# Branch A's gate product by blocks of two with seven products, its sums added in HBM

## The chip, the cores and the metric

The kernel runs on one core of a Trainium2 chip. The metric is the device time of one execution in microseconds (us). The core has engines that run beside one another, each through its own queue in order: TensorE (PE in the profile) multiplies matrices, VectorE (DVE) and ScalarE (ACT) work elementwise, GpSimd (POOL) does elementwise work too, and SyncE (SP) issues transfers (DMA) between HBM and on-chip memory. A matmul's result goes to PSUM, in banks of 128 x 512 floats; everything else lies in SBUF as tiles of 128 partitions.

## The reference

A two-layer backbone over 1024 latent tokens of 1024 channels (batch 1) and 256 context tokens. The even layer, which the change touches, is

```python
def even_mixer(h, h0, p):
    z = h @ p["w_in"]                       # 1024 -> 5 x 1024
    va, vg, ga, xb, gb = jnp.split(z, ...)
    y_a = conformer_conv(va, vg, p) * jax.nn.silu(ga)
    y_b, hT = rglru_branch(xb, p, h0, True)
    y_b = y_b * jax.nn.silu(gb)
    return jnp.concatenate([y_a, y_b], axis=-1) @ p["w_out"], hT
```

`conformer_conv` is a gate `va * sigmoid(vg)`, a depthwise convolution of width 31, a LayerNorm over the channels and a SiLU. `h` is the input after an RMS norm and a modulation. The odd layer (pooling mixer C) follows and is not changed. All is float32.

## The kernel before

Activations lie with channels on partitions: eight tiles of 128 channels x 1024 tokens, and each token half (512) is one PSUM bank. A float32 product is made of three matmuls of rounded operands: a number is split into a high part (`...h`, a cast on ACT to the format that PE reads) and a low part (`...l`, the difference, formed on POOL or DVE), and high x high, high x low and low x high are summed in one bank. `mm3_fixed` and `prod` are this loop over blocks of 128 channels.

The stages in order of the program: the condition and modulation sums; then eight *rounds*, one for each tile of channels, with the products `vg`, `va`, `xb` and the recurrence's gates on PE, the convolution on DVE, and the recurrence spread over DVE, ACT and POOL (`l` tiles); then the product `gb`; `wob`, the half of the output projection that reads branch B (eight output tiles x 48 matmuls); then `ga`, the gate of branch A, eight output tiles x two token halves x 24 matmuls; then `woa`, the half of the output projection that reads branch A, and the odd layer.

`woa` is already done by blocks of two with seven products (Strassen in Winograd's form): two output tiles, two halves of the contracted channels and two token halves form 2 x 2 blocks, and seven products of 12 matmuls take the place of eight. Its operands are called `b11`, `t1`, `t2`, `b21`, `t3`, `b22`, `t4`, its weights 1 to 7; sums and differences of activations (`ya`) and of weights are formed on DVE. Three banks `a`, `c`, `b` take the products, and bank `b` begins as a copy of bank `a` after product 1, made on ACT.

What sets the order: up to the flag `fixed[0] = False` the helpers `on`, `act`, `cast`, `vec` and `gp` tie each instruction to the one before on its engine, so that the order written out in the program is each engine's order. Their line in the profile is L670 (of the helper `on`). Behind the flag a scheduler orders by priority; `tc.high_priority(offset=EVAC)` moves an instruction ahead, `tc.issue_after` holds it behind another.

Around the change, before: in `wob`'s last two tiles ACT and DVE form the LayerNorm's sums (`mu`, `lsq`, `lnsum`); PE sums them over the channels with a matrix of ones (`ms_ln`); `ln_root` takes the root on ACT, `ln_scale` the reciprocal and eight scalings of `u` on DVE, `ln_silu` eight SiLUs on ACT, each for both token halves. The first two gate tiles (0 and 4) are written in the fixed order, with the row sum of half 1 behind the first of them; the other six follow in a loop (L161 to L163, L1428 to L1439) that multiplies the SiLU of the gate onto `u`, forms the operands of `woa`, and has the modulation sums of the second layer (`mods`, L1386) placed between. The weights' low parts of `ga` are formed on POOL, 128 x 1024 each.

## Time and profile before

| what | us |
|---|---|
| median of three runs | 1268.59 |
| lowest and highest run | 1265.97, 1269.95 |
| span of the profiled execution | 1263.6 |
| PE / DVE / ACT / POOL busy | 1249.8 / 1139.3 / 653.8 / 295.7 |
| gate product `ga` on PE, first to last start | 578.9 to 666.2 |

The span is that of one execution on the chip; the times of the runs have some 5 us around it. Rows of the timeline give start, duration, engine, source line, operation, output tile, input tiles, shapes and a count; in brackets stands how long the engine was idle before and for what. Groups give how often, the busy time and the mean in ns. Waits give total, times and longest. The granted clock of TensorE is full in all 40 slices.

### The profile page before, as it was taken

How to read it: one execution, taken by the hardware profiler on the slowest of the kernel's cores; microseconds unless marked ns; L12 is line 12 of the kernel's file. 1: busy time of each engine (PE TensorE's matmuls, PEld its weight loads, DVE VectorE, ACT ScalarE, POOL GpSimd, SP SyncE). 2: the span in 40 equal slices, each digit the busy share in tenths (PEclk: the TensorE clock that was granted, in tenths of full speed). 3: DMA queues.
4: the chain of work that ended last, by engine and by line, in shares of the span. 5: the costliest groups of instructions: out<-in, count | busy, mean ns of one | idle time of the engine just before them, and what ended most of it. 6: DMA issues, size and time to landing. Idle time of an engine off the chain costs nothing.

```text
span 1263.6 us, 16209 instructions
## 1 busy us (share of the span) xinstructions
PE 1249.8 (99%) x5866; PEld 1035.6 (82%) x5866; DVE 1139.3 (90%) x1746; ACT 653.8 (52%) x952; POOL 295.7 (23%) x176
## 2 busy tenths in 40 slices
PE   9999999999999999999999999999999999999997
PEld 7788888888888888888887878888888888888786
DVE  7799999999999999998978969999899987977975
ACT  8464566656666534237535445744343444644642
POOL 0015364436444547543210023000000000000002
PEclk9999999999999999999999999999999999999999
DMA  9970121112121233442436666344323334759723
GB/s 376 388 254 33 52 65 46 63 43 75 42 84 42 84 119 132 159 150 84 147 112 225 202 206 183 103 136 148 125 94 140 117 125 126 268 199 335 285 71 134
DMA packets 78705, 182.29 MB, mean 144 GB/s; under 512 B 7712, under 2 KB 23328, under 8 KB 78624
## 3 DMA queue, kind: packets, MB, share of 16 engines
q1 hardware_dynamic: 67328, 172.33, 39.8%
q10 hardware_dynamic: 11296, 8.92, 2.2%
q8 instruction: 46, 0.75, 0.2%
q14 instruction: 35, 0.29, 0.1%
HBM read 137.18 MB, written 44.04 MB: 143 GB/s over the span
## 4 chain that ended last, share of the span: by engine, by line
PE 70%; DVE 18%; DMA 7%; issue 2%; ACT 2%; POOL 1%; SPq 0%; POOLq 0%; ACTq 0%; DVEq 0%
PE wob L670 7%; DVE conv L670 5%; PE va L670 5%; PE xb L670 4%; PE vg L670 4%; DVE l L670 3%; PE fold L670 3%; PE g L670 3%; PE qb_v L1153 2%; PE ga L670 2%; PE qb_g L1156 2%; PE ga L161 2%; PE qb_v L1156 2%; PE qb_g L1155 2%; PE qb_g L1153 2%
## 5 line engine op out<-in xcount | busy, mean ns | idle before, releaser
L670 DVE SCALAR_TENSOR_TENSOR conv<-u,sm,conv 128x505 f32<-128x505 f32 (+6 forms) x224 | 153.6, 744 | 1.0
L2045 POOL TENSOR_TENSOR o<-x,rr 128x256 f32<-128x256 f32 (+1 forms) x10 | 9.2, 952 | 448.4 <-ACT rr L2045 448.4
L670 ACT ACTIVATE l<-g,sm 128x512 f32<-128x512 f32 (+1 forms) x96 | 58.7, 619 | 57.7 <-PE g L670 57.0
L670 POOL TENSOR_TENSOR l<-l,l 128x1280 f32<-128x1280 f32 x16 | 47.1, 2967 | 25.6 <-ACT l L670 15.1
L670 PE MATMUL gb<-h0h,wl_gb 128*128 128x512 f32 x128 | 49.9, 390 | 0.4 <-POOL wl_gb L670 0.4
L670 PE MATMUL va<-h0h,wl_va 128*128 128x512 f32 x128 | 49.9, 390 | 0.2 <-DVE wl_va L670 0.2
L98 ACT CAST wq_g<-wr_g 128x512 fp32r<-128x512 f32 x48 | 28.2, 621 | 41.9 <-DMA wr_g<-wg 15.6
L670 PE MATMUL gb<-h0l,wh_gb 128*128 128x512 f32 x128 | 49.8, 389 | 0.0
L670 PE MATMUL gb<-h0h,wh_gb 128*128 128x512 f32 x128 | 49.8, 389 | 0.0
L670 PE MATMUL va<-h0l,wh_va 128*128 128x512 f32 x128 | 49.8, 389 | 0.0
L670 PE MATMUL va<-h0h,wh_va 128*128 128x512 f32 x128 | 49.8, 389 | 0.0
L670 PE MATMUL wob<-ybl,wh_wob 128*128 128x512 f32 x128 | 49.8, 389 | 0.0
L670 PE MATMUL wob<-ybh,wl_wob 128*128 128x512 f32 x128 | 49.8, 389 | 0.0
L670 PE MATMUL wob<-ybh,wh_wob 128*128 128x512 f32 x128 | 49.8, 389 | 0.0
L670 DVE TENSOR_TENSOR_SCAN l<-l,l 128x256 f32<-128x256 f32 (+1 forms) x32 | 48.7, 1521 | 1.1
L670 DVE SCALAR_TENSOR_TENSOR conv<-cL,wsum,conv 128x506 f32<-128x506 f32 (+3 forms) x70 | 48.1, 745 | 0.2
L670 POOL TENSOR_TENSOR l<-l,uc 128x1280 f32<-128x1280 f32 x16 | 47.6, 2999 | 0.0
L98 ACT CAST wq_wo<-wr_wo 128x512 fp32r<-128x512 f32 x48 | 28.6, 620 | 35.5 <-DVE wr_wo L1134 12.4
L98 ACT CAST wq_v<-wr_v 128x512 fp32r<-128x512 f32 x48 | 28.1, 620 | 33.7 <-DMA wr_v<-wfold 16.6
L670 PE MATMUL xb<-h0l,wh_xb 128*128 128x512 f32 x112 | 43.8, 391 | 0.0
L670 PE MATMUL xb<-h0h,wh_xb 128*128 128x512 f32 x112 | 43.8, 391 | 0.0
L670 POOL TENSOR_TENSOR wl_xb<-wr_xb,wh_xb 128x1024 fp32r<-128x1024 f32 x7 | 16.8, 2407 | 114.5 <-ACT wh_xb L670 114.5
(680 smaller groups left out, 4362.5 us busy)
## 6 DMA issues: line engine op xcount, KB each, us to landing
modw<-modW SPq DMA_DIRECT2D x16, 512.0 KB, 10.2
mod<-modT SPq DMA_DIRECT2D x32, 256.0 KB, 3.4
wr_v<-wfold SPq DMA_DIRECT2D x16, 512.0 KB, 4.0
wr_g<-wg SPq DMA_DIRECT2D x16, 512.0 KB, 4.3
wr_wo<-wo SPq DMA_DIRECT2D x16, 512.0 KB, 4.1
mod<-modT SPq DMA_DIRECT2D x14, 512.0 KB, 4.5
y_b<-y SPq DMA_DIRECT2D x24, 256.0 KB, 3.5
y_t<-y SPq DMA_DIRECT2D x24, 256.0 KB, 3.1
```

What stands on the lines that cost most here:

```text
L98: return (nc.scalar.copy(hi, src), eng.tensor_tensor(out=lo, in0=src, in1=hi.bitcast(F32), op=sub))
L161: mm(ps, hi[:, kc], xh[k][:, cols], start=(k == 0), stop=False)
L670: last[eng] = f(*args, **kw)
L1153: nc.tensor.matmul(ps, hi, xh[k], start=(first and k == 0), stop=False, skip_group_check=not first)
L1155: nc.tensor.matmul(ps, hi, xl[k], start=False, stop=False, skip_group_check=not first)
L1156: mm = nc.tensor.matmul(ps, lo, xh[k], start=False, stop=(k == KH - 1), skip_group_check=not first)
L2045: tail[eng] = f(*args, **kw)
```

## The change

The gate product is now made in four rows q of two output tiles (q and q + 4) by seven products each. The activations' operands are `h` in halves of its channels and tokens and four sums of them (`t1` to `t4`), the weights three of `w_in`'s blocks and four sums.

*Sums in HBM.* They are formed by transfers in the rounds. SP copies the high parts of `h` to an HBM buffer `h_raw` (eight of 512 KB) in round 0; POOL issues eight transfers that add the low parts onto it, in rounds 0 and 1; in rounds 2 to 6 further copies and adding transfers (19 of POOL's in all) make `t1` to `t4` and the weight sums `wsum0` to `wsum3`. Four ACT operations negate two blocks. The only instructions that the rounds gain on compute engines are these four and POOL's transfers.

*Operands formed late.* In `wob`'s last tile and in the gate stage SP loads `t1` to `t4` (128 x 1024 tiles) and the weights (128 x 512 halves); ACT casts the high parts, 28 of weights and eight of `t`; low parts are made by POOL (28 of weights, four of `t`) and DVE (four of `t`).

*Products.* Of each row: 1 and 2 into bank `a` (with bank `b` copied from `a` between them), 5 into `c`, 6 into `b`, 3 into `c`, 7 into `b`, 4 into `b`; 4 stands within the next row, that of the last row behind the first product of `woa0`. Copies of `c` and `b` are kept in between and added on DVE.

*Moved.* The row sum of half 1 stands behind the first product of row 0; reciprocals, scalings and SiLUs of the LayerNorm stand between the first row's products; the modulation sums stand partly ahead of them. The operands of `woa` are written into the tiles of `h` after the last gate product has read them.

The core of the diff:

```diff
+GORDER = ([(0, p) for p in (1, 2, 5, 6, 3, 7)]
+          + [x for q in (1, 2, 3) for x in ((q, 1), (q, 2), (q - 1, 4), (q, 5), (q, 6), (q, 3), (q, 7))] + [(3, 4)])
...
+    def plus(dst, src):
+        on("pool", nc.gpsimd.dma_start, dst, src, accum_op=add, max_dma_last_dim=8192)
...
+    def sum_adds(j):
+        if j < 2:
+            for k in range(j * KH, (j + 1) * KH):
+                plus(h_raw[:, k * S : (k + 1) * S], plain(hl[k]))
...
-    for n, j in enumerate((0, KH)):
-        for h in range(2):
-            ga_product(j, gws[2 * KT + n], h)
-            if (n, h) == (0, 1):
-                ln_root(1, lnparts)
...
+    ga_product(0, 1, a, True, True)
+    ga_cast(3)
+    ga_low(3)
+    ln_root(1, lnparts)
+    cast(b, a)
+    for q in range(2):
+        t_cast("t2", q)
+        t_low("t2", q, None)
+    vec(nc.vector.reciprocal, out=lnr[0], in_=lnrt[0])
+    ga_product(0, 2, a, False, True)
...
+    ga_product(0, 5, c, True, True)
...
+    ln_scale(1, range(3))
+    vtt(out=a, in0=b, in1=ga_part[0, "c"], op=add)
+    ga_silu(a, 1)
+    ln_scale(1, range(3, KT))
+    for j in (0, KH, 1, KH + 1, 2, KH + 2, 3, KH + 3):
+        ln_silu(j, 1)
...
+    for q in range(1, KH):
...
+        ga_product(q, 1, a, True, True)
+        with tc.high_priority(offset=EVAC):
+            nc.scalar.copy(b, a)
...
+        ga_product(q, 2, a, False, True)
```

On PE, at the start of the gate stage, before: the last matmuls of the first gate tile's second half, the row sum of half 1 (`ms_ln`), and the next gate tile.

```order
L670 MATMUL ga_1_4997<-h0l_735,wh_ga_4860 128x512
L670 MATMUL ga_1_4997<-h0h_734,wl_ga_4861 128x512
L670 MATMUL ms_ln_5022<-mh_ln_4956,ones_r 128x512
L670 MATMUL ms_ln_5022<-ml_ln_4957,ones_r 128x512
L670 MATMUL ga_0_5027<-h0h_538,wh_ga_4968 128x512
```

And now: the end of product 1 of row 0 (bank `qa_ga`), the row sum, and product 2 into the same bank.

```order
L677 MATMUL qa_ga_5059<-h0l_630,wq_ga_4917 128x512
L677 MATMUL qa_ga_5059<-h0h_629,wq_ga_4917 128x512
L677 MATMUL ms_ln_5080<-mh_ln_5030,ones_r 128x512
L677 MATMUL ms_ln_5080<-ml_ln_5031,ones_r 128x512
L677 MATMUL qa_ga_5059<-h0h_713,wq_ga_4920 128x512
```

The row sum stood behind 48 gate matmuls and stands behind 12.

On ACT, in row 1 of the gate stage: the casts of `t4`, the second SiLU of row 0 (`qa_ga0`), the SiLUs of `u` in half 1, and the copy of bank `a` of row 1 (`qac_ga1_0`) into bank `b` (`qb_ga1`).

```order
L677 CAST h_t4h1_5051<-h_t4l1_5053 128x1024
L1399 CAST wq_ga10_5284<-wr_ga5_5238 128x512
L677 ACTIVATE qa_ga0_5059<-qa_ga0_5059 128x512
L677 ACTIVATE u0_1058<-u0_1058,sm_124 128x512
L677 ACTIVATE u4_2453<-u4_2453,sm_124 128x512
L677 ACTIVATE u1_1427<-u1_1427,sm_124 128x512
L677 ACTIVATE u5_2790<-u5_2790,sm_124 128x512
L677 ACTIVATE u2_1778<-u2_1778,sm_124 128x512
L677 ACTIVATE u6_3125<-u6_3125,sm_124 128x512
L677 ACTIVATE u3_2115<-u3_2115,sm_124 128x512
L1645 COPY qb_ga1_5224<-qac_ga1_0_5222 128x512
L677 ACTIVATE u7_3458<-u7_3458,sm_124 128x512
```

The copy is new; it stands behind seven of the eight SiLUs.

On DVE, in the first products of `woa0`, behind the last gate multiplication: low parts of `woa`'s operands (`h0l_3` is the last of t2, `h0l_7` the last of b21, in tiles that held `h`), of its weights (`wq_woa`), a difference, and an addition of a product onto `x1`.

```order
L106 TENSOR_TENSOR h0l_3_630<-u3_2115,h0h_3_629 128x512
L106 TENSOR_TENSOR ya_t3l1_5760<-u2_1778,ya_t3h1_5758 128x512
L106 TENSOR_TENSOR ya_t3l1_5760<-u3_2115,ya_t3h1_5758 128x512
L106 TENSOR_TENSOR ya_b22l0_5771<-u4_2453,ya_b22h0_5769 128x512
L106 TENSOR_TENSOR ya_b22l0_5771<-u5_2790,ya_b22h0_5769 128x512
L106 TENSOR_TENSOR ya_b22l1_5772<-u6_3125,ya_b22h1_5770 128x512
L106 TENSOR_TENSOR ya_b22l1_5772<-u7_3458,ya_b22h1_5770 128x512
L1616 TENSOR_TENSOR u3_2115<-u7_3458,u3_2115 128x512
L106 TENSOR_TENSOR wq_woa0_3_5751<-wr_woa0_0_5708,wq_woa0_3_5751 128x512
L1807 SCALAR_TENSOR_TENSOR x1_1_5788<-qc_woa0_5790,m0_141,x1_1_5788 128x512
L106 TENSOR_TENSOR wq_woa2_1_5869<-wr_woa2_0_5865,wq_woa2_1_5869 128x512
L106 TENSOR_TENSOR h0l_7_744<-u7_3458,h0h_7_743 128x512
```

Between the last low part of t2 and the last of b21 stand the low parts of t3 and b22 and the other work shown; before, the low parts of b21 were made within the gate stage, each behind its own gate tile.

More of the change, by code (lines that the diff above doesn't have):

```diff
@@ L1301, in ln_root, with ln_scale @@
         act(lnrt[h], ps, AF.Sqrt, bias=eps_l)
[L1303 to L1305 removed]
+    def ln_scale(h, tiles=range(KT)):
+        for j in tiles:
             v = us[j][:, HALF[h]]
@@ new lines, in ga_product, with ga_banks @@
+    def ga_product(q, p, ps, first, last_):
+        (wh, wl), (xh, xl) = ga_w[q, p], ga_operand(p)
+        for k in range(KH):
+            kc = slice(k * P, (k + 1) * P)
+            for t, (a, b) in enumerate(((wh, xh), (wh, xl), (wl, xh))):
+                on("pe", nc.tensor.matmul, ps, a[:, kc], b[k], start=(first and k == 0 and t == 0),
+                   stop=(last_ and k == KH - 1 and t == 2), skip_group_check=not first)
+    ga_bank, ga_part = {}, {}
+    def ga_banks(q):
+        if q % 2:
+            a, c = banks(f"qac_ga{q}", 0)
+            b = wide(f"qb_ga{q}")[:, HALF[1]]
+        else:
+            a, c, b = [psum(f"q{n}_ga{q}") for n in "acb"]
+        ga_bank[q] = a, c, b
@@ new lines, in body @@
+    ga_product(0, 6, b, False, True)
+    ln_scale(0)
+    t_low("t3", 1, vtt)
+    ga_keep(0, "b", b)
+    for j in range(KT):
+        ln_silu(j, 0)
+    ga_product(0, 3, c, False, True)
+    ga_gate(0, 0, 0, a)
+    ga_op(6)
+    ga_op(7)
+    ga_raw(4)
+    vec(nc.vector.reciprocal, out=lnr[1], in_=lnrt[1])
+    vtt(out=c, in0=c, in1=ga_part[0, "b"], op=add)
+    ga_silu(c, 0)
+    ga_product(0, 7, b, False, True)
+    for q in range(2):
+        t_cast("t4", q)
+        t_low("t4", q, gp)
```

301 lines of the change are left out of this document (240 added, 61 removed).

## The prediction

> **What bounds the kernel now.** I read the page first, then the waits of PE, then the groups that touch the tile `ga`.
>
> ```profile
> span 1263.6 us, 16209 instructions
> ...
> PE 1249.8 (99%) x5866; PEld 1035.6 (82%) x5866; DVE 1139.3 (90%) x1746; ACT 653.8 (52%) x952; POOL 295.7 (23%) x176
> ...
> PE 70%; DVE 18%; DMA 7%; issue 2%; ACT 2%; POOL 1%; SPq 0%; POOLq 0%; ACTq 0%; DVEq 0%
> ```
>
> TensorE is busy for 99% of the span. The list of its waits shows how little is left: the four longest are
>
> ```profile
> PE fin_ms L2045 <- DVE dg L2045: 1.2, 1, 1.2
> PE warm L140 <- DVE eps_r L182: 1.1, 1, 1.1
> PE qc_wo L1155 <- DVE y_b22l L99: 0.9, 1, 0.9
> PE qc_woa L1153 <- ACT wq_woa L98: 0.8, 1, 0.8
> ```
>
> So a matmul removed is time removed, and a wait added on PE is time added: there is no idle stretch behind it that could take it up. The gate product of branch A is this stage:
>
> ```profile
> L163 PE MATMUL ga<-h0h,wl_ga x96: 389/389/389, 601.6 to 666.2; 128*128 128x512 f32 x96
> ...
> L670 PE MATMUL ga<-h0h,wh_ga x32: 389/389/397, 578.9 to 600.5; 128*128 128x512 f32 x32
> ...
> 654.63 0.39 PE L163 MATMUL ga<-h0h,wl_ga 128*128 128x512 f32 x1
> 654.86 0.39 PE L161 MATMUL ga<-h0h,wh_ga 128*128 128x512 f32 x1
> ```
>
> The 0.39 us is how long one matmul lasts; they start 0.23 us apart. From 578.9 to 666.2 stand 384 of them (two more for a row sum): 87.3/385 = 0.227 us each. A product of 12 takes 2.7 us.
>
> **What it removes.** Each of the four rows now has seven products of 12, 336 matmuls instead of 384. The changed order has them all, so this is certain: 48 x 0.227 = -10.9 us.
>
> **What it adds on PE's path.** I walk the changed order with the durations of before, on before's clock; PE enters the stage at 578.9 in both. These rows of ACT and DVE carry it:
>
> ```profile
> 584.61 0.69 ACT L670 ACTIVATE sq_ln<-ms_ln,eps_l 128x512 f32<-128x512 f32 x1
> 585.19 0.61 ACT L670 CAST mh_ln<-lnsum 128x512 fp32r<-128x512 f32 x1
> 585.70 0.69 ACT L670 ACTIVATE wo<-wob,m 128x512 f32<-128x512 f32 x1
> 586.28 1.04 ACT L670 CAST wh_ga<-wr_ga 128x1024 fp32r<-128x1024 f32 x1
> ...
> 592.68 0.58 ACT L670 ACTIVATE ga<-ga 128x512 f32<-128x512 f32 x1
> 593.18 5.75 ACT L670 ACTIVATE u<-u,sm 128x512 f32<-128x512 f32 x8
> ...
> 669.34 0.57 ACT L1496 COPY qb_woa<-qa_woa 128x512 f32<-128x512 f32 x1 [1.25 <-PE qa_woa L1156]
> ...
> 585.84 0.69 DVE L670 TENSOR_TENSOR ml_ln<-lnsum,mh_ln 128x512 fp32r<-128x512 f32 x1 [1.44 <-ACT mh_ln L670]
> 586.44 3.35 DVE L670 RECIPROCAL ms_ln<-sq_ln 128x512 f32<-128x512 f32 x1
> 589.83 4.87 DVE L670 TENSOR_TENSOR u<-u,ms_ln 128x512 f32<-128x512 f32 x8
> 594.62 0.68 DVE L670 TENSOR_TENSOR u<-u,ga 128x512 f32<-128x512 f32 x1
> ...
> 645.97 0.68 DVE L1386 SCALAR_TENSOR_TENSOR mod<-mod,cH 128x512 f32<-128x512 f32 x1
> ...
> 646.59 0.68 DVE L1386 SCALAR_TENSOR_TENSOR mod<-mod,cH 128x512 f32<-128x512 f32 x1
> ...
> L119 DVE TENSOR_TENSOR wl<-wr,wh 128x1024 fp32r<-128x1024 f32 x9 | 11.0, 1223 | 5.0 <-ACT wh L119 4.9
> ```
>
> In a row of such instructions one ends 0.52 us (ACT) or 0.60 us (DVE) after the one before for 128x512, 0.95 and 1.2 us for 128x1024, 0.72 us for a SiLU of u (5.75/8).
>
> 1. *The row sum of half 1.* Before it stood after 48 gate matmuls, at 589.8; now it stands after 12, at 581.6. Its operands are formed by 585.8 (ACT) and 586.5 (DVE), and nothing in the change forms them earlier: 4.9 us of wait. What hid it was the 36 matmuls between.
> 2. *The first copy of bank a into bank b.* Product 2 goes into the same bank behind product 1, so PE waits for the copy. On ACT stand ahead of it the two casts of t1 (1.9), a `wo` (0.6), two weight casts (1.0) and a root (0.6), all after 585.8: the copy ends at 590.5, PE could have gone on at 587.0: 3.5 us.
> 3. *Row 0's last product.* DVE forms two low parts of t2 behind ACT (591.5 to 593.9), the reciprocal (597.3), two modulation sums (598.6), eight scales (603.4) and the second low part of t3 (604.6). PE, with four products from 590.5, is half through product 7 at 602.8: 1.8 us. The next weights wait behind the eight SiLUs on ACT and a 1.3 us split on POOL: 1.0 us.
> 4. *The copy of row 1.* PE ends product 1 of row 1 at 609.8. Its copy stands on ACT behind the second SiLU of row 0 and seven SiLUs of half 1. DVE from 604.6: three sums (606.4), gate (607.0), second reciprocal (610.4), an addition, three sums, a split, three scales (615.2), the addition the second SiLU waits for (615.8). ACT: that SiLU to 616.4, seven to 621.4, copy to 622.0. 12.2 us, the largest term.
> 5. *Copies of rows 2 and 3* have no queue ahead: 0.57 and two hand-overs, 0.9 each, 1.8 us, and 0.3 at the last product.
> 6. *The operands of `woa0`.* DVE has no room there:
>
> ```profile
> 601.00:667.00 66.00, 66.00 (x293) 54.66 (x292) 56.22 (x102) 29.76 (x49) 12.93 (x5) 1.00 0.39 125
> 667.00:690.00 23.00, 22.23 (x99) 18.13 (x98) 22.76 (x37) 13.70 (x26) 0.00 (x0) 1.00 0.75 238
> ```
>
> (The fourth pair is DVE: 56.2 of 66 us, then 22.8 of 23.) From product 3 of row 3 to the last low part of t2, DVE has some 24 instructions, 14.4 us; PE meanwhile has product 7, a `woa0` product, product 4 and three quarters of the next, 10.2 us: wait 4.2. Then 12 more DVE instructions (7.3 us) to the last low part of b21 against 2.7 us of matmuls: 4.6. Together 8.8 us, less the 0.8 us that PE waits at `qc_woa` today.
>
> Waits: 4.9+3.5+1.8+1.0+12.2+1.8+0.3+8.8-0.8 = 33.5 us. The modulation sums that move ahead give DVE room behind `woa0`, but PE hardly waits there now, so that is worth nothing.
>
> **What has no row.** POOL now issues 19 adding transfers; none is in the trace of before. Four of 512 KB stand in round 0 ahead of `wl_va`:
>
> ```profile
> 118.99 5.89 POOL L670 TENSOR_TENSOR l<-l,uc 128x1280 f32<-128x1280 f32 x2
> 124.85 2.41 POOL L670 TENSOR_TENSOR wl_va<-wr_va,wh_va 128x1024 fp32r<-128x1024 f32 x1
> ...
> 159.16 2.41 POOL L670 TENSOR_TENSOR wl_vg<-wr_vg,wh_vg 128x1024 fp32r<-128x1024 f32 x1 [14.35 <-DVE conv L670]
> ...
> 130.37 0.39 PE L670 MATMUL va<-h0h,wl_va 128*128 128x512 f32 x1
> ...
> 91.17 0.33 SPq L698 DMA_DIRECT2D wr_vg<-win  x1
> ...
> wr_v<-wfold SPq DMA_DIRECT2D x16, 512.0 KB, 4.0
> ```
>
> PE reads `wl_va` at 130.4, 3.1 us after it is formed. If an issue on POOL takes what SP's takes (0.33), the four cost 1.3 us and are hidden: 0. If POOL is held for a transfer's whole landing, 4 x 4.0 - 3.1 = +12.9. Round 1's four stand in the 14.35 us that POOL idles. A gain is excluded: nothing there gets earlier. An issue is nearest to the issue's row: I take 0, and keep +12.9. SP's added copies wait for those adds ahead of round 2's loads; the same 14.35 us covers 3.6 us for each add. The Trainium skill, page "DMA: Bandwidth & Descriptors", section "Anatomy of one DMA — SWDGE (gpsimd) path", puts a GpSimd transfer at 2.0 us plus its bytes at 436 GB/s, mostly completion and not issue; its estimate for 512 KB is 3.2 us, under the 4.0 us row, and the sum by it would still lie between my two ends. No run here shows it yet.
>
> POOL also makes 28 weight splits and four 1024-wide ones beside DVE. One DVE row shows DVE held by such a split, another not:
>
> ```profile
> 613.17 2.88 POOL L99 TENSOR_TENSOR wl_ga<-wr_ga,wh_ga 128x1024 fp32r<-128x1024 f32 x1 [8.46 <-ACT wh_ga L98]
> ...
> 613.71 2.89 DVE L1386 SCALAR_TENSOR_TENSOR mod<-mod,cH 128x512 f32<-128x512 f32 x1
> ...
> 122.33 1.28 DVE L670 SCALAR_TENSOR_TENSOR uc<-xb,sm,uc 128x1023 f32<-128x1023 f32 x1
> ...
> 572.67 1.30 POOL L670 TENSOR_TENSOR xp<-xp,wo 128x512 f32<-128x512 f32 x1 [8.96 <-ACT wo L670]
> ```
>
> The modulation sum, 0.68 us elsewhere, lasts until POOL's split is over; the `uc` at 122.33 has its usual 1.28 us beside POOL's product of 118.99. In step 4's chain stand eight splits of 1.30 and two of 2.40, 15.2 us. Lower end 0, upper end 15.2; I take 2 (three of the splits meeting such an instruction half way).
>
> **Sum.** -10.9 + 33.5 + 0 + 2 = +24.6 us. The profiled execution is 1263.6 us and the median of the runs 1268.6, 5.0 above it, which lies around the span; I add to both alike: 1288.2 and 1293 us.
>
> **Rivals.**
> - *POOL holds DVE throughout* (price above): +15.2 instead of +2, about 1306 us. For it the row at 613.71, against it the `uc` row. The Trainium skill, page "SBUF — State Buffer", section "SBUF: two separate sides", says that a DVE instruction with two SBUF inputs and a GpSimd instruction that reads SBUF exclude each other for a whole instruction. The trace agrees at 613.71 and not at 122.33. Chance 0.17.
> - *POOL is held by its adding transfers* in round 0: +12.9, about 1306 us. For and against it no row speaks but the 0.33 us of SP. Chance 0.10.
> - *Faster: ACT and DVE come early enough.* The place is the copy of row 1. If the whole LayerNorm work of steps 1 to 4 ran 12.2 us earlier, its copy would be made when PE's product 1 ends (609.8); the waits of steps 1 to 4 would be gone, and that of step 6, which is the same backlog; 1.8+0.3 remain: -10.9+2.1 = -8.8, about 1260 us. It decides where all waits together fall under 7 us (10.9 less 4). For it: DVE idles 15% of 601 to 667. Against it: both queues are served in order, and the chain starts at a cast (585.19) that the change leaves alone. Chance 0.12.
> - *No change:* two thirds of the waits of steps 1 to 6 go and the rest (about 11 us) just pays for the 10.9. Chance 0.06.
> - That the matmuls are not saved has no chance, as the order shows.
>
> **How the numbers follow.** The forecast itself has 0.55: waits of 22 to 45 us, 1280 to 1303. A run tells a difference of about 0.3% (4 us) from none. Faster 0.12, same 0.06, slower 0.82. The range takes in the forecast and both slower rivals: 1268 to 1312; the faster case lies outside.
>
> **What would show it.** PE's waits in the changed profile: `ms_ln` on DVE some 5 us, `qa_ga` on ACT 3 to 4, `qac_ga` on ACT's copy about 12, `qc_woa` and `qb_woa` on `h0l` about 9; the stage should have 336 gate matmuls and end some 14 us later at its last product. If `qac_ga` waits under 3 us, step 4 is wrong, and the sign may be. If PE waits for `wl_va` in round 1, the transfers hold POOL; if DVE's scales and sums grow past 1 us beside POOL's splits, POOL holds DVE.

## The result, and the profile after

| | before | after |
|---|---|---|
| median of the runs, us | 1269.0 | 1312.94 (1305.67 to 1313.9) |
| span of the profiled execution, us | 1263.6 | 1311.1 |

The changed kernel takes 1.034 times as long (95% interval 1.031 to 1.037). The prediction was 1293 us with a range of 1268 to 1312: slower, as forecast, but by 44 us instead of 24, just outside the range. Each run's time lies 1.8 us above its own span (1312.86 and 1311.1 us), not some 5: the profiled execution of before was about 3 us faster than the median of its runs.

The page of the changed kernel, to be held against the first lines of the prediction:

```profile
span 1311.1 us, 16367 instructions
...
PE 1256.7 (96%) x5818; PEld 1034.1 (79%) x5818; DVE 1158.6 (88%) x1758; ACT 678.4 (52%) x996; POOL 343.8 (26%) x219
...
PE 54%; DVE 28%; DMA 8%; issue 5%; ACT 3%; POOL 2%; SPq 0%; POOLq 0%; DVEq 0%; ACTq 0%
```

PE has 48 matmuls fewer and yet 6.9 us more busy time; its idle time rose from 13.8 to 54.4 us; and DVE's share of the chain that ended last went from 18% to 28%. The list of PE's waits in the changed kernel (total, times, longest):

```profile
PE qac_ga L677 <- ACT qb_ga L1645: 15.1, 2, 14.4
PE ms_ln L677 <- ACT mh_ln L677: 4.2, 1, 4.2
PE va L677 <- ACT wh_va L677: 3.6, 1, 3.6
PE va L677 <- POOL wl_va L677: 3.3, 3, 1.6
PE qa_ga L677 <- ACT qb_ga L677: 3.1, 1, 3.1
PE qc_woa L1225 <- DVE h0l L106: 3.0, 1, 3.0
PE qb_ga L677 <- DVE h_t3l L677: 2.5, 1, 2.5
```

Two of them (`va`) belong to the rounds, the others to the gate stage. Where the time came in is read from when two groups of matmuls end: the last of `wob`, ahead of the gate stage, and the last of `fin_ms`, at the program's end. First the two groups of before, then of after (count, durations in ns, first and last start):

```profile
L670 PE MATMUL wob<-ybl,wh_wob x128: 389/389/395, 490.7 to 578.0; 128*128 128x512 f32 x128
L2045 PE MATMUL fin_ms<-dg,ones x6: 377/416/697, 1243.1 to 1256.4; 128*128 128x256 f32 x4, 128*128 128x512 f32 x2
```

```profile
L677 PE MATMUL wob<-ybl,wh_wob x128: 389/389/389, 502.9 to 590.2; 128*128 128x512 f32 x128
L2315 PE MATMUL fin_ms<-dg,ones x6: 377/416/697, 1290.2 to 1303.5; 128*128 128x256 f32 x4, 128*128 128x512 f32 x2
```

`wob` ends 12.2 us late (590.2 - 578.0), the program 47.1 us (1303.5 - 1256.4). So **12.2 us are lost in the rounds and 34.9 us behind them**, most of them in the gate stage and the first `woa` products: `woa`'s last matmul starts 44.0 us late (788.2 - 744.2), so 31.8 us are lost up to there and 3.1 in the odd layer. Since the execution of before was a fast one, 47.1 us is some 3 us more than the medians' 44.

### The profile page after: what moved, and what is told of

Same layout as the page of the kernel before. It is cut to its first block, busy times and chain, and to the rows that moved or that the text cites. A ratio compares the mean times of both kernels' runs of the same rounds, so it can differ in the third digit from the quotient of the medians.

```text
span 1311.1 us, 16367 instructions
## 1 busy us (share of the span) xinstructions
PE 1256.7 (96%) x5818; PEld 1034.1 (79%) x5818; DVE 1158.6 (88%) x1758; ACT 678.4 (52%) x996; POOL 343.8 (26%) x219
## 4 chain that ended last, share of the span: by engine, by line
PE 54%; DVE 28%; DMA 8%; issue 5%; ACT 3%; POOL 2%; SPq 0%; POOLq 0%; DVEq 0%; ACTq 0%
DVE conv L677 8%; PE wob L677 5%; DVE l L677 5%; PE va L677 3%; PE fold L677 3%; PE xb L677 3%; DVE u L677 2%; PE g L677 2%; DMA modw<-modW 2%; PE vg L677 2%; PE qb_v L1223 1%; PE qb_v L1225 1%; PE qb_ga L677 1%; PE qb_v L1226 1%; PE qb_g L1225 1%
## 5 line engine op out<-in xcount | busy, mean ns | idle before, releaser
L677 POOL TENSOR_TENSOR l<-l,l 128x1280 f32<-128x1280 f32 x16 | 47.1, 2968 | 30.9 <-ACT l L677 27.4
L105 ACT CAST wq_v<-wr_v 128x512 fp32r<-128x512 f32 x48 | 28.1, 620 | 42.0 <-DMA wr_v<-wfold 19.2
L105 ACT CAST wq_wo<-wr_wo 128x512 fp32r<-128x512 f32 x48 | 28.7, 619 | 39.5 <-DMA wr_wo<-wo 11.9
```

Source lines behind the costliest of these rows:

```text
L105: return (nc.scalar.copy(hi, src), eng.tensor_tensor(out=lo, in0=src, in1=hi.bitcast(F32), op=sub))
L677: last[eng] = f(*args, **kw)
```

## The experiments

Sixteen more kernels ran, beside runs of the kernel before on the same chip. Late at `wob` and late at the end are the two differences above, taken from each kernel's own groups; the last column is their difference, called the gate stage's loss below.

| kernel | median, us | ratio to before (95%) | `wob` late | end late | gate stage |
|---|---|---|---|---|---|
| after | 1312.94 | 1.034 (1.031-1.037) | 12.2 | 47.1 | 34.9 |
| e1_rounds | 1303.37 | 1.029 (1.027-1.031) | 1.2 | 37.5 | 36.3 |
| e4b_rounds | 1322.51 | 1.042 (1.040-1.044) | 22.5 | 59.2 | 36.7 |
| e8_rounds | 1322.34 | 1.043 (1.040-1.045) | 21.0 | 56.5 | 35.5 |
| e14_rounds | 1303.31 | 1.028 (1.026-1.030) | 0.6 | 36.5 | 35.9 |
| e3_nosums | 1301.75 | 1.028 (1.026-1.029) | 1.2 | 35.2 | 34.0 |
| e2_copy | 1313.65 | 1.037 (1.035-1.038) | 8.7 | 49.6 | 40.9 |
| e5_bank | 1309.42 | 1.031 (1.029-1.034) | 7.4 | 44.0 | 36.6 |
| e11_fill | 1309.92 | 1.034 (1.032-1.035) | 9.7 | 45.7 | 36.0 |
| e12_nomods | 1302.87 | 1.027 (1.025-1.029) | 9.3 | 37.0 | 27.7 |
| e13_nolow | 1304.18 | 1.028 (1.025-1.030) | 10.0 | 38.1 | 28.1 |
| e7_rows | 1303.87 | 1.027 (1.025-1.029) | 22.5 | 37.5 | 15.0 |
| e9_rows | 1304.81 | 1.029 (1.027-1.030) | 18.9 | 39.8 | 20.9 |
| e10_nomods | 1295.19 | 1.022 (1.021-1.024) | 18.0 | 28.9 | 10.9 |
| e15_rows | 1282.39 | 1.011 (1.009-1.013) | 0.4 | 16.7 | 16.3 |
| e4_waits (on before) | 1315.62 | 1.039 (1.037-1.041) | 47.8 | 50.3 | 2.5 |
| e6_lock (on before) | 1275.45 | 1.005 (1.003-1.007) | 1.0 | 6.6 | 5.6 |

Kernels with the same rounds as the changed one are late by 7.4 to 12.2 us at `wob`; so times of those are compared by the last column, not by the median. Each row rests on one execution, and all are held against the same one of before. The column repeats within some 2 us where only the rounds differ: the changed gate stage gives 34.9 to 36.7 in after, e1, e4b, e8 and e14. That of e7_rows gives 15.0, 16.3 and 20.9, but 14.3, 14.8 and 16.7 where it is read at the end of `woa`; the rest is the odd layer's.

### The rounds: a queue

In the trace of the changed kernel, SP's queue in round 1 (start, duration, engine, line, operation), the ACT instruction and the PE matmul behind it:

```profile
140.60 25.07 SPq L841 DMA_DIRECT2D n<-h_raw  x4
165.72 0.55 SPq L843 DMA_DIRECT2D h_t<-h_raw  x1
166.36 0.58 SPq L948 DMA_DIRECT2D yb_raw<-l  x1
...
175.97 1.36 ACT L677 ACTIVATE l<-l,chalf 128x1280 f32<-128x1280 f32 x1 [9.65 <-DMA yb_raw<-l]
...
178.31 0.79 PE L677 MATMUL va<-h0h,wh_va 128*128 128x512 f32 x1 [3.62 <-ACT wh_va L677]
```

and in before, and POOL's adds in the changed kernel:

```profile
156.34 0.33 SPq L880 DMA_DIRECT2D yb_raw<-l  x1
...
162.82 2.61 ACT L670 ACTIVATE l<-l,chalf 128x1280 f32<-128x1280 f32 x2
```

```profile
150.66 3.52 POOL L677 DMA_DIRECT2D h_raw<-h0l  x4
```

SP holds four loads of `h_raw` for 25 us, until POOL's adds of 150.66 have landed (9.3 us from issue to landing, the median in the list of transfers). The store of the recurrence stands behind them and goes out 10 us late; ACT may overwrite the stored tile `l` only after it, and the cast of `va`'s weights stands behind ACT's instruction. In round 4 the same happens behind the copy of a weight sum, and in round 0 PE waits a little for POOL, whose four adds stand ahead of `wl_va`:

```profile
307.07 1.37 ACT L677 ACTIVATE l<-l,chalf 128x1280 f32<-128x1280 f32 x1 [5.62 <-DMA yb_raw<-l]
...
132.38 0.50 PE L677 MATMUL va<-h0h,wl_va 128*128 128x512 f32 x1 [0.53 <-POOL wl_va L677]
```

Held against before matmul by matmul, PE is 1.3 us late ahead of the first round already, loses 0.8 in round 0, 7.7 in round 1 (waits of 3.6 and 1.2 and slower matmuls behind them) and 1.9 in round 4; 0.5 come later. The first experiment moves the copies behind the store (`sum_copies` from the load of `va` to behind `rec_sum`) and the adds to `h_raw` into round 1; the four negations move to round 3. Some of its sums miss an add, so its values differ.

```diff
                 wva = raw_split(raw_load(win[j], f"va{j}"), f"va{j}")
-                sum_copies(j)
...
                 rec_sum(state)
+                sum_copies(j)
...
-            for k in range(j * KH, (j + 1) * KH):
+            for k in range(KT) if j else ():
                 plus(h_raw[:, k * S : (k + 1) * S], plain(hl[k]))
```

> The changed kernel with SP's copies of the sums issued in each round behind the store of yb_raw instead of ahead of it, and all eight of POOL's adds onto h_raw in round 1, where POOL idles, instead of four of them ahead of wl_va. Theory: in the rounds PE loses 10.4 us because SP's copies wait for POOL's adds to land, the store of the recurrence's tile stands behind them, and ACT waits for that store. Then the last va starts 2 to 4 us later than before instead of 11.7, and the time is about 1304. Rival: the loss comes from the traffic itself (the DMA engines are full at 172 us) or from POOL's time at its issues; then the shift stays over 8 us and the time within 3 us of 1313.

`wob` is 1.2 us late instead of 12.2, with all the transfers still issued. The edit moves POOL's adds as well as SP's copies; that the order on SP cost most is read from the waits above, where 9.6 us come behind the store and 0.8 behind POOL. e4b_rounds keeps that order and has every sum:

```diff
         elif j == 3:
+            for t in neg["12"] + neg["21"]:
+                act(t, t, AF.Identity, scale=-1.0)
             for n in ("t1", "t3"):
...
-        elif j == 4:
+        elif j == 5:
             plus(blocks(h_ops["t2"]), h_rows[:, KH:, HALF[1]])
...
-        elif j == 5:
+        elif j == 6:
             for q in range(2):
                 plus(h_ops["t4"][:, q * S : (q + 1) * S], neg["21"][q])
```

> The changed kernel with its transfers rearranged in the rounds only: the copies among the scratch buffers are issued on SP behind the store of the recurrence (yb_raw) instead of ahead of it, all eight adds to h_raw stand in round 1, and the later sums move a round each (negated quarters, t1 and t3 in round 3, t2 and the third weight sum in round 5, t4 and the last in round 6). All sums are formed. Theory (rounds, the order on SP): the store no longer waits for POOL's adds to land; the last value product, 11.7 us late in the changed kernel, is under 2 us late; 1301 to 1305 us. Rival (the adds on POOL and the traffic themselves cost): the last value product stays over 5 us late and the time over 1308.

The theory missed: 22.5 us late and 1322.51 us are what the rival forecast, though not for its reason, as e14_rounds will show. Suspected was one copy on SP, and e8_rounds moves the add that it waits for a round ahead:

```diff
+        elif j == 4:
+            plus(wsums[2], ga_rows[1][1])
         elif j == 5:
             plus(blocks(h_ops["t2"]), h_rows[:, KH:, HALF[1]])
-            plus(wsums[2], ga_rows[1][1])
```

> The kernel of e4b_rounds with one add moved: the add to the third weight sum goes from round 5 to round 4, so that no copy that waits for an add of the round before stands ahead of a store of the recurrence on SP. All sums are formed. Theory (the order on SP alone makes the rounds late): the last value product is under 1.5 us late, the last product of the second output weights (wob) too, and the time is 1300 to 1305. Rival (traffic or POOL's issues): the rounds stay over 5 us late, and the time over 1307.

The theory missed again, 21.0 us late, where the rival had it, but the trace shows another wait. DVE's product of `va` in the same round, first in e8_rounds, then in e14_rounds below:

```profile
364.15 0.69 DVE L677 TENSOR_TENSOR u<-va,sg 128x512 f32<-128x512 f32 x1 [12.69 <-issue]
```

```profile
350.84 0.68 DVE L677 TENSOR_TENSOR u<-va,sg 128x512 f32<-128x512 f32 x1
```

The tile `u` takes the buffer of a negated quarter (`n`), whose add to `t4` I had put off into round 6, where it is issued at 357.7. e14_rounds uses up all negated quarters in round 3:

```diff
                 nc.sync.dma_start(blocks(h_ops["t3"]), h_rows[:, KH:, HALF[1]])
+                nc.sync.dma_start(blocks(h_ops["t4"]), h_rows[:, KH:, HALF[1]])
...
-            for n in ("t1", "t3"):
+            for n, x in (("t1", "12"), ("t3", "12"), ("t4", "21")):
                 for q in range(2):
-                    plus(h_ops[n][:, q * S : (q + 1) * S], neg["12"][q])
+                    plus(h_ops[n][:, q * S : (q + 1) * S], neg[x][q])
...
+            plus(h_ops["t4"], h_ops["t1"])
```

> The changed kernel with the transfers of the rounds in another order, all sums formed: copies on SP behind the store of the recurrence, the adds to h_raw all in round 1, and t4 begun as a copy of the last quarter in round 2, so that all negated quarters are used up in round 3 (their buffers go to the tiles u of rounds 5 to 7, for which VectorE waited in e4b_rounds and e8_rounds); t1 is added to t4 in round 5. Theory (the order on SP and, in the two kernels before, these buffers made the rounds late): the last wob product is under 1.5 us late, and the time 1300 to 1305. Rival (the traffic of the sums): over 5 us late, over 1306.

0.6 us late with all sums formed, and the store is in its old place:

```profile
178.55 2.62 SPq L841 DMA_DIRECT2D n<-h_raw  x4
...
156.40 0.33 SPq L947 DMA_DIRECT2D yb_raw<-l  x1
```

The rival, the traffic of the sums, fails here. So the sums in HBM cost nothing that these runs can tell; what cost was the place of their copies in SP's queue, and in e4b_rounds and e8_rounds the late use of a buffer. The counterpart leaves the sums out (loads read other blocks, so values differ):

```diff
     def sum_copies(j):
+        return
...
     def sum_adds(j):
+        return
```

> The changed kernel without the sums in HBM: no copies and no adding transfers in the rounds; the gate stage loads plain blocks of win and of yb_raw in their place, with the same shapes, so that the gate's values are others. Theory: all of the 10.4 us that the rounds lose come from these transfers, the gate stage stays as it is: about 1302, the last va within 1.5 us of the shift that the kernel starts with (1.3). Rival: the gate stage also waits for loads of sums that land late; then more than 13 us are won.

1301.75 us against 1303.31 with all sums: the intervals overlap, and the gate stage alone loses 34.0.

### The gate stage: is it the copy, and its bank?

e2_copy puts the first product of row 1 and its copy ahead of LayerNorm's scales and SiLUs of half 1:

```diff
+    ga_banks(1)
+    ga_product(1, 1, ga_bank[1][0], True, True)
+    cast(ga_bank[1][2], ga_bank[1][0])
     ln_scale(1, range(3))
```

> The changed kernel with product 1 of row 1 and its copy of bank a into b ahead of the second SiLU of row 0 and the SiLUs of half 1 on ACT. Theory: the 14.4 us wait is the copy's place in ACT's queue; the wait falls to about 1 us, the slow clock behind it goes too (2 to 3 us), and the time is 1296 to 1300. Rival: the LayerNorm work is late anyway and holds PE at a later place (products 4 and 7, or the operands of woa0), so that under 5 us are won: 1308 or more.

Nothing is won: the medians are alike, and the stage loses 40.9 us instead of 34.9. The longest wait is still

```profile
PE qac_ga L677 <- ACT qb_ga L677: 11.9, 1, 11.9
```

because bank `b` of row 1 is a half of the wide PSUM tile that holds the reciprocal of half 1, which the scales read. e5_bank gives it a bank of its own:

```diff
-            b = wide(f"qb_ga{q}")[:, HALF[1]]
+            b = psum(f"qb_ga{q}") if q == 1 else wide(f"qb_ga{q}")[:, HALF[1]]
```

> The kernel of e2_copy, with bank b of row 1 taken from a PSUM bank of its own instead of the half of the wide tile that holds the reciprocal of LayerNorm's second half. Theory (the bank was the cause): the copy of row 1's first product need not wait for the last scale of that half; the wait of row 1 (11.9 us there, 14.4 in the changed kernel) falls to 1 to 5 us, and the time to 1304 to 1308, since some of the wait returns at the fourth product and at the copies of later rows. Rival (the late work of LayerNorm on DVE holds TensorE in any case): the wait only moves to the next instructions, less than 3 us is won, 1310 to 1314.

The wait is gone from row 1 (3.4 us left) and stands at the next row's copy, as the rival said; the stage loses 36.6, and the time of 1309.42 us lies between the two forecasts:

```profile
PE qa_ga L677 <- ACT qb_ga L1650: 8.5, 1, 8.5
```

### The gate stage: is it the clock behind a wait?

Behind its waits the changed kernel's matmuls stand 0.43 us apart instead of 0.23. To see from which wait on, e4_waits gives five tiles of `wob` in the kernel before an idle product that waits for 2, 4, 7, 12 and 24 passes of ACT over its bank:

```diff
+        if m in (1, 2, 3, 4, 5):
+            on("pe", nc.tensor.matmul, wob_ps[m][0], w[0][:, :P], bh[0][:, HALF[0]], start=True, stop=True)
+            for _ in range({1: 2, 2: 4, 3: 7, 4: 12, 5: 24}[m]):
+                act(wob_ps[m][0], wob_ps[m][0], AF.Identity)
```

> The kernel before with five waits put into the product wob, tiles 1 to 5: one more matmul into the bank, 2, 4, 7, 12 and 24 passes of ACT over that bank, then the bank's own products, which overwrite it; the result stays. Waits of about 1.4, 2.5, 4.0, 6.6 and 13 us, 27.5 in all. Theory: a wait beyond some 3 us halves TensorE's clock, and it stays halved for about 5 us of work after it, so the matmuls behind the three long waits stand 0.43 us apart for a stretch that costs 2 to 3 us each: in all 27.5 + 1 + 8 = +36 us, about 1305. Rival: the slower matmuls of the changed kernel come from its transfers or from what the other engines do; then the matmuls here keep 0.227 us and the time is about 1297.

The passes took longer than planned; the waits were 2.65, 3.87, 5.71, 8.78 and 16.14 us. Matmuls behind the first three:

```profile
504.28 0.50 PE L670 MATMUL wob<-ybh,wh_wob 128*128 128x512 f32 x1 [2.65 <-ACT wob L670]
504.62 0.39 PE L670 MATMUL wob<-ybl,wh_wob 128*128 128x512 f32 x1
...
520.13 0.60 PE L670 MATMUL wob<-ybh,wl_wob 128*128 128x512 f32 x1
520.52 0.63 PE L670 MATMUL wob<-ybh,wh_wob 128*128 128x512 f32 x1
520.95 0.63 PE L670 MATMUL wob<-ybl,wh_wob 128*128 128x512 f32 x1
...
538.30 0.79 PE L670 MATMUL wob<-ybh,wh_wob 128*128 128x512 f32 x1 [5.71 <-ACT wob L670]
538.89 0.63 PE L670 MATMUL wob<-ybl,wh_wob 128*128 128x512 f32 x1
539.32 0.63 PE L670 MATMUL wob<-ybh,wl_wob 128*128 128x512 f32 x1
```

After 2.65 us nothing changes; from 3.87 us on, 7 to 13 matmuls follow at 0.43 us (520.13 to 523.51, 538.30 to 544.01, 561.15 to 564.30, 590.24 to 595.09), with a granted clock of 0.50 to 0.53 in the stretches of 520 and 538, however long the wait was. Some 39 of them at 0.2 us are 8 us beside 37.2 us of waits. So the slower spacing follows waits, without the changed kernel's transfers. But 2.65 us is no safe length: in the changed kernel a wait of 2.5 us was followed, 1.4 us later, by matmuls at 0.43 us with a granted clock of 0.51 (622 to 625 us), and in e6_lock below waits of 0.6 and 1.7 us close together were too (660.9 to 663.8).

```profile
620.43 0.50 PE L677 MATMUL qb_ga<-h_t3l,wq_ga 128*128 128x512 f32 x1 [2.52 <-DVE h_t3l L677]
...
622.23 0.63 PE L677 MATMUL qac_ga<-h0l,wq_ga 128*128 128x512 f32 x1
```

Is that on the path? e11_fill puts idle products into four waits of the changed kernel's gate stage, so that the clock stays up:

```diff
+    idle_pe(16)
     ln_root(1, lnparts)
...
+    idle_pe(12)
     ga_product(0, 2, a, False, True)
...
+    idle_pe(9)
     ga_product(0, 7, b, False, True)
...
+        if q == 1:
+            idle_pe(60)
         ga_product(q, 2, a, False, True)
```

> The changed kernel with products that feed nothing in four waits of the gate stage: 16 ahead of the row sum of LayerNorm's second half, 12 ahead of the second product of row 0, 9 ahead of its seventh, 60 ahead of the second product of row 1 (128x512 each, 0.23 us at full clock, a little less than each wait), in a PSUM bank of their own. Theory (the lower clock behind a wait costs time of its own): no stretch of matmuls 0.43 us apart is left behind these waits; what the earlier three win is lost again in the wait of row 1, which VectorE's last scale sets, and behind that one 2 to 3 us stay won: 1308 to 1311. Second theory (the whole of the lower clock is on the path): 7 to 10 us are won, 1302 to 1306. Rival (the spacing is no clock, but something that the operands do): the stretches stay and nothing is won, 1312 to 1316.

Matmuls behind the filled waits of row 0 run at full spacing, behind row 1's only a short stretch is slow (640.5 to 643.1), and the stage loses 36.0 us, no less than without (34.9). Even the 2 to 3 us behind row 1 are not kept: in `woa0` PE, come earlier, waits for the same DVE instructions (3.0 and 1.9 us, 3.0 and 1.6 in the changed kernel). So the time that the lower clock takes is time that PE would have waited for another engine. The median, 1309.92, lies in the first theory's range, but `wob` is 2.5 us less late here than in the changed kernel.

### The gate stage: VectorE, and POOL beside it

DVE is nearly without a pause there in the changed kernel (a window of 40 us; busy time and count of PE, weight loads, DVE, ACT, POOL; granted clock, DMA share, GB/s):

```profile
600.00:640.00 40.00, 21.07 (x72) 16.01 (x72) 38.82 (x49) 27.22 (x41) 25.37 (x14) 0.71 0.53 177
```

and in before:

```profile
600.00:640.00 40.00, 40.00 (x178) 33.13 (x177) 36.95 (x64) 18.47 (x28) 10.53 (x4) 1.00 0.46 155
```

38.8 of 40 us with 49 instructions, against 37.0 us with 64. Its instructions are longer. e13_nolow leaves out POOL's 28 splits of gate weights; the third product of a group takes the high part again, which doubles that part of the gate (the expectation's "small part" was wrong).

```diff
     def ga_low(n):
         hi, lo = ga_w[GORDER[n]]
-        (gp if fixed[0] else nc.gpsimd.tensor_tensor)(out=lo, in0=ga_src[n], in1=plain(hi), op=sub)
+        return
...
-            for t, (a, b) in enumerate(((wh, xh), (wh, xl), (wl, xh))):
+            for t, (a, b) in enumerate(((wh, xh), (wh, xl), (wh, xh))):
```

> The changed kernel without POOL's 28 subtractions that form the low parts of the gate weights; each third product of a group takes the high part again, so the gate products lack a small part. TensorE, ScalarE and VectorE have the instructions of the changed kernel. Theory (POOL's splits hold VectorE, which sets the gate stage): VectorE's additions and scales between 600 and 640 us have their own lengths again (0.68 us for 128x512, 1.2 for 128x1024), and of the stage's 35 us 6 to 12 go: 1300 to 1307. Rival (the stretched instructions stand in time that VectorE would wait anyway): under 3 us go, 1310 to 1314.

DVE's row sum of half 1 (`ml_ln`), the same five instructions behind it, and POOL beside them, in the changed kernel:

```profile
598.16 0.69 DVE L677 TENSOR_TENSOR ml_ln<-lnsum,mh_ln 128x512 fp32r<-128x512 f32 x1 [1.43 <-ACT mh_ln L677]
603.72 4.54 DVE L677 SCALAR_TENSOR_TENSOR h_t2l<-h_t2l,h_t2h 128x1024 fp32r<-128x1024 f32 x2 [1.13 <-ACT h_t2h L677]
...
612.68 1.76 DVE L1580 SCALAR_TENSOR_TENSOR mod<-mod,cH 128x512 f32<-128x512 f32 x1
...
629.46 2.83 DVE L106 TENSOR_TENSOR h0l<-u,h0h 128x512 fp32r<-128x512 f32 x1
...
634.60 3.06 DVE L677 TENSOR_TENSOR u<-u,ms_ln 128x512 f32<-128x512 f32 x5
...
603.69 5.73 POOL L677 TENSOR_TENSOR wq_ga<-wr_ga,wq_ga 128x512 fp32r<-128x512 f32 x3
```

and in e13_nolow:

```profile
595.92 0.69 DVE L677 TENSOR_TENSOR ml_ln<-lnsum,mh_ln 128x512 fp32r<-128x512 f32 x1 [1.43 <-ACT mh_ln L677]
...
601.48 2.36 DVE L677 SCALAR_TENSOR_TENSOR h_t2l<-h_t2l,h_t2h 128x1024 fp32r<-128x1024 f32 x2 [1.13 <-ACT h_t2h L677]
...
607.62 0.69 DVE L1580 SCALAR_TENSOR_TENSOR mod<-mod,cH 128x512 f32<-128x512 f32 x1
...
621.66 0.68 DVE L106 TENSOR_TENSOR h0l<-u,h0h 128x512 fp32r<-128x512 f32 x1
...
624.66 3.06 DVE L677 TENSOR_TENSOR u<-u,ms_ln 128x512 f32<-128x512 f32 x5
```

From `ml_ln` to the last scales DVE takes 36.4 us (634.60 - 598.16) and without POOL's splits 28.7 (624.66 - 595.92). Of these 7.7 us, 0.6 are a modulation sum that the scheduler placed in this stretch only in the changed kernel; the other 7.1 are longer instructions: 2.2 in the low parts of `t2`, 2.8 in three modulation sums, 2.1 in `h0l`. So **POOL holds DVE for 7.1 us** in this chain, and the stage loses 28.1 instead of 34.9. (`h0l` stands beside POOL's low parts of `t4`, which e13_nolow keeps; there they come 2.2 us after `h0l`.) PE itself waits for none of POOL's splits in the changed kernel's gate stage. The scales `u<-u,ms_ln` have one input in PSUM and the same length in both; three of them run beside a split of POOL's in the changed kernel (632.21) and take 1.87 us there as in e13_nolow.

e6_lock asks the same of the kernel before: 16 additions on POOL that feed nothing.

```diff
+    with tc.issue_after(t2_low.ins):
+        idle_ = vtile("idle_pool")
+        nc.gpsimd.memset(idle_, 0.0)
+        for _ in range(16):
+            nc.gpsimd.tensor_tensor(out=idle_, in0=idle_, in1=idle_, op=add)
```

> The kernel before, with sixteen additions of a tile of its own (128x512 fp32, two inputs in SBUF) on POOL behind the low part of t2 in the last product, where POOL is idle and DVE busy to the end; they feed nothing. Theory (POOL and DVE exclude each other where both read two operands from SBUF): DVE's instructions beside them are stretched, TensorE waits for DVE's operands, and the time rises by 8 to 20 us, to 1277 to 1289. Rival (no such exclusion; the stretched rows of the changed kernel come from something else): DVE's rows beside the additions have their lengths of before, and the time is within 3 us of before, 1266 to 1272.

The scheduler ran them earlier than meant, from 591.6 to 621.4 us. An instruction of DVE's beside them, then one with the same line in before:

```profile
611.45 1.52 DVE L1436 TENSOR_TENSOR yat<-u,u 128x512 f32<-128x512 f32 x1
```

```profile
627.62 0.69 DVE L1436 TENSOR_TENSOR yat<-u,u 128x512 f32<-128x512 f32 x1
```

The hold is there, and the time rises by 7.0 us in the medians, between the two forecasts. PE waits for no operand of DVE's in that stage: in the profiled execution it loses 4.4 us from 656 to 664 us, in waits of 0.6 and 1.7 us for a gate weight, whose cast stands on ACT behind one that waits for DVE, and at half the clock behind them. Why it is under the 8 to 20 us expected is not shown. e12_nomods then takes load from DVE in the changed kernel: 32 modulation sums, which the gate stage holds before and after alike.

```diff
-                    nc.vector.scalar_tensor_tensor(out=raw, in0=raw, scalar=1.0, in1=cH, op0=mult, op1=mult,
-                                                   accum_out=m1p[:, n, q : q + 1])
+                    nc.gpsimd.tensor_copy(m1p[:, n, q : q + 1], raw[:, :1])
```

> The changed kernel without the 32 multiply-and-sum instructions of the later modulation on VectorE (single columns copied by POOL in their place, so that modulation has other values). Theory (VectorE's load bounds the gate stage: in the kernel of e9_rows, relieved of the same instructions, 10 of 20.9 us went): between the last wob product and the end, the changed kernel loses 35 us; 8 to 15 of them go, and the time is 1298 to 1305. Rival (in the changed kernel the chains of the first two rows set the end, before these instructions matter): under 4 us go, 1309 to 1314.

The stage loses 27.7 instead of 34.9; 7.2 us, a little under the 8 expected. DVE's stretch from `ml_ln` to the last scales, which held eight of the sums, takes 26.1 us (621.39 - 595.26). The wait of row 1 falls in both experiments; here it is

```profile
PE qac_ga L677 <- ACT qb_ga L1644: 5.3, 2, 4.6
```

(the longest of the two; 14.4 us in the changed kernel, 9.3 in e13_nolow).

### Another order

e7_rows starts rows 0 and 1 together, each hiding the other's copy; e9_rows and e15_rows put the same gate stage behind the rounds of e8_rounds and e14_rounds.

```diff
-GORDER = ([(0, p) for p in (1, 2, 5, 6, 3, 7)]
-          + [x for q in (1, 2, 3) for x in ((q, 1), (q, 2), (q - 1, 4), (q, 5), (q, 6), (q, 3), (q, 7))] + [(3, 4)])
+GORDER = ([(0, 1), (1, 1), (0, 2), (1, 2), (0, 5), (0, 6), (0, 3), (0, 7), (1, 5), (0, 4), (1, 6), (1, 3), (1, 7)]
+          + [x for q in (2, 3) for x in ((q, 1), (q - 1, 4), (q, 2), (q, 5), (q, 6), (q, 3), (q, 7))] + [(3, 4)])
...
+                    ga_product(1, 1, first_a, True, True)
+                    cast(ga_bank[1][2], first_a)
+                    ga_product(0, 2, a, False, True)
+                    ga_product(1, 2, first_a, False, True)
```

> The kernel of e4b_rounds with another order in the gate stage: rows 0 and 1 begin together (their first and second products stand ahead of the row sum of LayerNorm's second half, so that each copy is hidden behind the other row's products), the copies go first on ACT, the first reciprocal is ahead of the second half's row sum on DVE, row 1 takes banks that do not hold a reciprocal, product 4 stands between the first two products of the next row, and the first operands of row 3 are formed ahead of the modulations. Theory (what the gate stage lost is wait and the clock behind it, not the products): its three large waits (4.2, 3.1 and 14.4 us) fall under 2 us each, and the time is 1266 to 1280. Rival (the evictions, splits and copies on ACT and DVE bound the stage, and POOL's splits hold DVE): the waits return at the later rows and the last product, and the time stays 1288 to 1303.

Its rounds were those of e4b_rounds, 22.5 us late, so neither theory's time could come; the stage itself loses 15.0 instead of about 35.

> The gate stage of e7_rows behind the rounds of e8_rounds; all of the result is computed. Theory (the two losses stand one behind the other and add up): e7's 21 us that came from its rounds go, its gate stage keeps its 15, and the time is 1280 to 1287. Rival (the gate stage absorbs some of what the rounds lose): over 1290.

The time is the rival's, 1304.81 us, but for the rounds' defect, 18.9 us; the stage loses 20.9, of which 4.2 stand behind `woa`. e10_nomods is e9_rows without the modulation sums (the diff of e12_nomods):

> The kernel of e9_rows without the 32 multiply-and-sum instructions of the later modulation on VectorE (0.69 us each and 0.08 for the read of the sum, 24.6 us in all); single columns copied by POOL stand in their place, so that modulation has other values. Theory (VectorE's capacity between the last wob product and the end of woa0 bounds the gate stage once TensorE has less to do there): of the 15 us that the stage of e9_rows loses, 7 to 12 go, and the time is 1270 to 1277. Rival (the chains between TensorE, ScalarE and VectorE bound it, not the load): under 4 us go, over 1278.

The time is where the rival had it, 1295.19 us, but because of the rounds; the stage, which the theory is about, loses 10.9 instead of 20.9, and 7.0 instead of 16.7 at the end of `woa`.

> The gate stage of e9_rows behind the rounds of e14_rounds, all of the result computed. Theory (losses of the rounds and of the gate stage add up, and the gate stage is bounded by VectorE's load): nothing is lost in the rounds, 15 to 21 us in the gate stage, and the time is 1283 to 1290. Rival: the gate stage, begun earlier, meets other work and loses more, 1291 to 1304.

1282.39 us, just under the theory's range, all computed, 30 us under the changed kernel and 13.7 above the one before. Its longest waits are for DVE:

```profile
PE qbc_ga L677 <- DVE qa_ga L731: 4.1, 1, 4.1
PE qb_ga L677 <- DVE m L1589: 3.2, 1, 3.2
PE qc_woa L1222 <- DVE x L1860: 2.7, 1, 2.7
```

No version beat the kernel before.

## Why the prediction was right in sign and short by 20 us

| step of the sum | forecast, us | measured, us |
|---|---|---|
| 48 matmuls fewer | -10.9 | they are gone |
| 1 row sum of half 1 | 4.9 | 4.2 |
| 2 first copy | 3.5 | 3.1 |
| 3 last product of row 0 | 1.8 + 1.0 | 2.5 |
| 4 copy of row 1 | 12.2 | 14.4 |
| 5 copies of rows 2 and 3, last product | 1.8 + 0.3 | 0.7 + 0.7 |
| 6 operands of `woa0`, less 0.8 | 8.0 | 5.6 (0.9 + 3.0 + 1.6 + 0.9, less 0.8) |
| adding transfers in the rounds | 0 | 12.2, 1.3 of them ahead of the rounds |
| POOL beside DVE | 2 | 7.1, within the waits above |

**The waits.** Walking the changed order with the durations of before gave all six waits, each at the place forecast: 33.5 us in all, 31.2 measured. This is why the sign was right, and the rival that ACT and DVE come early enough fell with the wait of row 1. That the sizes agree so well is partly luck: POOL's hold lengthened the measured waits, and matmuls at half the clock filled part of them. Without POOL's weight splits the wait of row 1 is 9.3 us (e13_nolow), under the 12.2 forecast for that case. Counted on PE, the matmuls that are gone (-10.9), the waits (31.2) and the half clock (about 8.5) make 28.8 of the 31.8 us at the end of `woa`.

**The transfers** are the step that failed: the term of 0 for the adding transfers measured 12.2 us at `wob`, 9.6 of them because the recurrence's store was held in SP's queue. The text asked what POOL's adds do to POOL, and took 0.33 us for an issue; it was 0.9 (3.52 us for four), and in round 0, where four stand ahead of `wl_va`, PE lost 0.8 us. For SP it checked only the loads behind the copies ("the same 14.35 us covers 3.6 us for each add"). The store of the recurrence stands in the same queue, frees a tile of ACT's, and was not named; an add lands after 9.3 us, not 4.0. The rival that POOL is held for a landing had nearly the right price (12.9) by luck: it was on the wrong queue, as the 0.5 us wait for `wl_va` in round 0 shows. With the copies behind the store, e1_rounds and e14_rounds lose 0.6 to 1.2 us.

**POOL beside DVE** was a rival with 0.17 and a term of 2 us; it is real, at half the rival's price of 15.2 (7.1 us of DVE's time, 6.8 at the end). The counterexample in the prediction, `uc<-xb,sm,uc`, was misread: `xb` is in PSUM, so that only one of the two tiles that it reads lies in SBUF; it does not speak against the rival. Of the rows read from 598 to 640 us, those with two inputs in SBUF beside a split of POOL's are stretched, as the modulation sum of before is, and the scales with one input in PSUM are not. The rule of the Trainium skill, "SBUF — State Buffer", section "SBUF: two separate sides", thus agrees with all of them, the `uc` row included.

**What no step had.** Matmuls at half the clock behind waits (5.2, 3.2, 4.4 and 4.9 us of them from 602 to 717 us in the changed kernel, about 8.5 us lost on PE, and some 2 us more in round 1) explain most of why PE is busy longer with fewer matmuls. They are not a loss of their own: e11_fill removed nearly all of the first three and the stage lost as much. Bank `b` of row 1 under the reciprocal was overlooked in step 4, and e2_copy and e5_bank show that it, too, only decides where PE waits. And in step 6 the late operands were called t2 and b21; by their tiles they are those of t1 and t2, which changes no number.

**What sets the gate stage.** Two ways of relieving DVE there gained 6.8 and 7.2 us in the changed kernel and 10.0 in the other order; three ways of relieving PE or moving a copy (e11_fill, e2_copy, e5_bank) gained nothing. So DVE's chain to the last scales sets a part of it, with POOL's hold in that chain. After either relief 27.7 to 28.1 us are still lost, and the other order of the same work (e15_rows) took off more, some 19 us; which of its several moves did it was not tried singly. The change frees 10.9 us on PE and adds 19.3 us to DVE's busy time (1158.6 - 1139.3), the hold included, in a stage where DVE had 3 of 40 us to spare. Of the 10.3 us by which the stage missed its forecast (34.9 against 24.6), about 5 are POOL's hold beyond the 2 forecast (7.1 on DVE, 6.8 at the end), and 3.1 came in behind `woa`, in the odd layer; the rest is not assigned.

## What to carry to other kernels

When an engine shows 99%, look at the second one in the stage that changes: here DVE was at 92% of it, and products saved on TensorE were paid for in elementwise work. Loads that waited on SP held the store behind them for 10 us: name the stores behind a transfer that will wait and who reuses their tiles, before counting bytes. And take an engine's durations with its neighbour's load: splits given to POOL came back as longer instructions on DVE.

## What the hardware showed that I had not expected

- In e4_waits TensorE's granted clock is 0.50 to 0.53 behind waits of 3.87 and 5.71 us and 1.00 behind 2.65; matmuls stay at half speed for 3.2 to 5.7 us, and the length of the wait made no difference up to 16.1 us. The Trainium skill, "TensorE: Matmul & The Clock Gate", section "Part 1: The HAM clock gate (the "warmup" mystery)", gives half the clock after an idle window of about 3.4 us until a busy one of that length. These five waits agree with the first length, and the slow stretches lie around the second; the wait of 2.5 us in the changed kernel, with half the clock 1.4 us behind it, does not agree with the first.
- A 128x512 instruction of DVE's with two inputs in SBUF took up to 2.83 us instead of 0.68 beside POOL's splits, and 1.52 beside a row of POOL's additions.
- An adding transfer of 512 KB took 0.9 us of POOL and landed after 9.3 us where four were issued in a row, after 14.1 with eight (e1_rounds; medians); a plain copy of that size between the same places, issued by SP in a row of eight, landed after 8.0.
